# A hybrid decoder layer on one core: seven-product blocks for attention's projections, and attention moved beside pooling

## The chip, the cores and the metric

The kernel runs on one core of a Trainium2 chip. The metric is device time in microseconds (us), the median of several runs. A NeuronCore has five engines, each with its own queue in order: TensorE (PE in the profile; PEld is its weight load), VectorE (DVE), ScalarE (ACT), GpSimd (POOL) and SyncE (SP), which here issues the loads. Tiles lie in on-chip memory (SBUF, and PSUM for TensorE's sums); DRAM is reached by DMA.

## The reference, cut to what matters

One layer, 512 positions, model width 2048, float32:

```
h    = rms_norm(x) * norm_g
proj = h @ w_in            # columns: z_ssd 2048 | x 2048, B 512, C 512 | dt 32 | u_pool 2048 | z_pool 2048
                           #          | q 1536 | k 1536 | v 1536 | z_attn 512 | gate logits 3 x 2048
y_ssd  = ssd_branch(z_ssd, conv(x,B,C), dt, ...)                # convolution, SiLU, chunked scan, gated norm
y_pool = (pooled(u) - u) @ pool_w * pool_scale * silu(z_pool)   # causal means, windows 2, 4, 8, 16, one per group
y_attn = combine(attn(q,k,v) of 3 groups) * silu(z_attn)        # 4 heads of 128 per group, windows of 128 keys, dilation 1, 4, 16
merged = sigmoid(g0) * (y_ssd @ w_br_ssd) + sigmoid(g1) * (y_pool @ w_br_pool) + sigmoid(g2) * (y_attn @ w_br_attn)
x = x + merged @ w_out
out = x + sigmoid((rms_norm(x) * ple_norm_g) @ w_ple_gate) * (p @ w_ple_proj)
```

## The kernel before

**Precision.** Every large product is made of three matmuls in the fast float32 form. A value is split into `hi` (rounded by a copy on ScalarE, L136) and `lo`, the remainder (a subtraction on VectorE, L137); hi x hi, hi x lo and lo x hi are added in PSUM (`product`, L146). The weights are loaded as `raw` tiles of 128 x 1024 values (512 KB), three buffers deep, split, and used at once. `h` is kept transposed and split in `HT` (`hh`, `hl`) for most of the run.

**Entries, jobs and ticks.** `plan` lists all weight tiles in the order of use, an entry each; `jobs` lists the products. `split(n)` (L116) emits the split of all entries up to n and, for each, the load of the entry three further on. A job asks for the split of the entry two ahead, emits the 24 matmuls of its own entry (12 in a seven-product block), evacuates PSUM after its last entry, and calls `tick()`. `tick` (L84) takes one step of the generator at the head of `tasks` and one of the generator at the head of `other`; in this way vector work and small matmuls are laid between the large ones, in an order written out by hand. `flush()` (L89) ticks until both queues are empty, with no large matmuls between. `job_a` (L151) makes 128 positions x 512 columns with `h` as the stationary operand, `job_b` (L179) the transposed form. 512 columns over a depth of 2048 are 16 x 4 x 3 = 192 matmuls of 512 columns in either.

**Seven-product blocks** (`s_block`, L251). 1,024 columns of `w_in` are treated as a 2 x 2 block product with seven products in place of eight (Strassen's scheme in Winograd's form), 7 x 48 = 336 matmuls instead of 384. `make_left` (L226) makes the four left-hand sums S1 to S4 of `h` once, in two halves, most of it on VectorE, and one sum per half on GpSimd (L239). The right-hand sums (T2 and T3, T1, T4) are made from the raw weights on VectorE (L274, L276, L280, L283) when an entry is split, just before its rounding copy. There are three passes over the depth: (a, T2, T3), (d, T1), (c, T4); after each, `after` (L309) adds the products in `st` tiles, and calls `evac`. For the gates that is a sigmoid on ScalarE (L551) and a store from ScalarE's queue (L553) into `gate_d`.

**Order of the stages.** (1) `start`, norm and transposition of x, beside the product p @ w_ple_proj. (2) `enter` (L556) takes SBUF for the blocks (`swap`), steps `make_left`; six seven-product blocks for the gate logits; then the SBUF goes back to the pool of 52 general tiles (`T`). (3) `load_columns` (L413): per-channel vectors, nine small loads from GpSimd, two of them (L422) of `d_skip`, element by element. (4) For each of three groups q, k, v by `job_a`; norm and transposition of q and k (`qk_norm`) and the core (`attn_core`, L626: for each block of 128 queries a score step, a transposition step and a value step) run as tasks beside the following products. (5) dt, B and C with the causal convolution in `conv_evac` (L796), `dt_task`, `ssd_prep`, and the combination of the groups (`combine`, L744). (6) x of the SSD, scan (`ssd_core`), z of the SSD, z of attention (`za_evac`) beside the norm `y_norm` (L1050). (7) The SSD's merge, four `job_a`, then group 0 of pooling, attention's merge (`merge_att`, after a flush) and the rest of pooling (`pool_group`, L1137; sums in `pooled`). (8) Split of pooling's result (`yp_split`), pooling's merge, output projection, last gate, output.

The change and the prediction touch the helpers `tick`, `flush`, `split`, `make_left` and `s_block`, the stages 2 to 5, and the order in 6 to 8.

Of the kernel before, what the change touches and what calls it, by code (L numbers as in the profile page):

```python
# [9 lines left out]
F32 = mybir.dt.float32  # L10
# [7 lines left out]
L = 512  # L18
# [13 lines left out]
def hybrid_kernel(ctx: ExitStack, tc: tile.TileContext, x, p, norm_g, w_in, conv_w, conv_b, dt_bias, a_log,  # L32
# [40 lines left out]
    tasks, other = deque(), deque()  # L73
# [42 lines left out]
    def split(n):  # L116
        while state["split"] <= n and state["split"] < len(plan):
# [4 lines left out]
            if callable(plan[i]):  # L122
                r, k, c = plan[i]("raw"), 2, L
            else:
                r = raws.pop(i)
                _, k, c = plan[i]
# [6 lines left out]
            else:  # L133
                hi = wp.tile([128, k, c], F32R, name="hi", tag="hi")
                lo = wp.tile([128, k, c], F32R, name="lo", tag="lo")
                A.copy(hi, r)  # L136
                (G if 1 < i < EARLY else V).tensor_tensor(lo, r, hi.bitcast(F32), op=ALU.subtract)  # L137
# [88 lines left out]
    def make_left():  # L226
# [8 lines left out]
        for q0 in (0, 4):  # L235
            x = {}
            for n in ("L11", "L21", "L22", "L12"):
                x[n] = sp.tile([128, 4, 256], F32, name="x4", tag="t2", bufs=4)
                (G if n == "L12" else V).tensor_tensor(x[n], part(0, n), part(1, n), op=ALU.add)  # L239
            x["S3"] = sp.tile([128, 4, 256], F32, name="x4", tag="rs", bufs=2)  # L240
            V.tensor_sub(x["S3"], x["L11"], x["L21"])
            V.tensor_add(x["L22"], x["L21"], x["L22"])
            V.tensor_sub(x["L11"], x["L22"], x["L11"])
            V.tensor_sub(x["L12"], x["L12"], x["L11"])
            for n, o in (("S2", "L11"), ("S3", "S3"), ("S4", "L12"), ("S1", "L22")):
# [3 lines left out]
            yield  # L249

    def s_block(c0, evac):  # L251
# [15 lines left out]
        def entry(name, e, loads):  # L267
            def f(what):
# [3 lines left out]
                elif what == "raw":  # L272
                    if name == "T2":
# [3 lines left out]
                        raw["T2", e], raw["T3", e] = t, raw.pop(("b", e))  # L277
                        raw.pop(("a", e)), raw.pop(("d", e))
                    elif name == "T1":
                        V.tensor_sub(raw["d", e], raw["d", e], raw["T2", e])  # L280
                        return raw["d", e]
                    elif name == "T4":
                        V.tensor_sub(raw["T2", e], raw["T2", e], raw["c", e])  # L283
                        return raw["T2", e]
                    return raw[name, e]
                elif name in ("T3", "T1", "T4", "c"):
                    raw.pop(({"T1": "d", "T4": "T2"}.get(name, name), e))
                    if name == "T4":
                        raw.pop(("c", e), None)
            if name == "c":  # L290
                keep = f

                def f(what):
                    if what != "done":
                        return keep(what)
# [10 lines left out]
        def tile_():  # L306
            return held["sp"].tile([128, L], F32, name="st", tag="st", bufs=8)

        def after(name):  # L309
            for t in range(2):  # L310
                p = ps[name][t]
                if name == "L11":
                    st["u2", t] = tile_()
# [3 lines left out]
                elif name == "S3":  # L317
                    st["u3", t] = tile_()
# [3 lines left out]
                elif name == "S1":  # L322
                    o = tile_()
# [4 lines left out]
                elif name == "L12":  # L328
                    evac(t, 0, p, tile_())
# [83 lines left out]
    def load_columns():  # L413
# [10 lines left out]
        yield  # L424
        yield
# [14 lines left out]
    gb = []  # L440
# [7 lines left out]
    def start():  # L448
# [30 lines left out]
        load_xt(3)  # L479

# [63 lines left out]
    hook(flush)  # L544


    gate_d = dram.tile([3, L, D], F32, name="gate_d")

# [6 lines left out]

    def enter():  # L556
        swap("sp")
        load(state["split"])
        split(state["split"])
        tasks.append(make_left())  # L560
        step(tasks)

    hook(enter)
    for br in (0, 2, 1):
# [3 lines left out]
    hook(lambda: tasks.append(load_columns()))  # L568
# [23 lines left out]
    def qk_evac(raw, ss):  # L592
        def f(t, ps):
            q, sq = T("q"), T("sq")
            A.copy(q, ps)
            G.tensor_tensor(sq, q, q, op=ALU.mult)
            V.tensor_reduce(ss[:, 4 * t:4 * t + 4], sq.rearrange("q (h d) -> q h d", h=4), axis=AX.X, op=ALU.add)
            raw[t] = q
        return f
# [26 lines left out]
    def attn_core(gi, t0):  # L626
        yield from fresh(t0, 2)
# [65 lines left out]
        if gi == 2:  # L693
            other.append(combine())

    sm_mx = sm(4)
# [6 lines left out]

    def v_perm(gi):
        def f(kt, t):
            if gi == 0:
                return hkt(kt, t)
            return tuple(HT[i][:, kt].rearrange("q (i r) -> q r i", r=4)[:, t] for i in range(2))
        return f

    def v_evac(gi):
        def f(t, ps):
            v = T("v")
            if t % 2:
                V.tensor_copy(v, ps)
            else:
                A.copy(v, ps)
            vv[gi, t] = v
        return f

    def attention(gi):
        rq, rk = {}, {}
        job_a(w_in, QO + gi * L, 16, hkt, qk_evac(rq, ss16),
              post=lambda: tasks.append(qk_norm(gi, rq, ss16, rt16, scr16, qT, False)))
        job_a(w_in, KO + gi * L, 16, hkt, qk_evac(rk, ss16b),
              post=lambda: tasks.append(qk_norm(gi, rk, ss16b, rt16b, scr16b, kT, True)))
        job_a(w_in, VO + gi * L, 16, v_perm(gi), v_evac(gi), post=lambda: tasks.append(attn_core(gi, now["t"])))

    for gi in range(3):
        attention(gi)  # L730

    za_d = dram.tile([4, 128, L], F32, name="za_d")
    ya_d = dram.tile([4, 128, L], F32, name="ya_d")

    def za_evac(j):
        def f(n, ps):
            z = T("za")
            A.activation(z, ps, AF.Silu)
            nc.scalar.dma_start(out=za_d[2 * j + n], in_=z)
        return f  # L740
# [576 lines left out]
```

## Time and profile before

| | |
|---|---|
| median of 3 runs | 2753.78 us (2751.42 to 2754.65) |
| the profiled execution | 2756.26 us; its span, first to last instruction, 2753.4 us |
| mean granted TensorE clock | 0.986 |
| 1,024 columns of gates (336 matmuls), one block | 83.8 to 84.0 us |
| VectorE, ScalarE, GpSimd busy | 49%, 34%, 8% of the span |
| DMA | 326.5 MB, mean 119 GB/s |

How to read the rows: a row of the timeline gives start, duration, engine, source line, operation, output <- input, shapes, and in brackets the engine's idle time before it and what ended that. A row of the view by windows gives a stretch, then the busy time and the number of instructions of each engine, the granted clock (PEclk, 1.00 is full), the DMA engines' busy share and GB/s. A row of the view of waits gives who waited for whom, the sum in us, how many times, and the longest. In a row of the view by lines, what stands before the bar is line, engine, operation, tiles, shapes and count; behind it come busy time, mean ns of one, and the idle time before. A row of DMA issues gives their count, the KB of each, and the median us to landing.

### The profile page before, as it was taken

Reading aid. Unit: us, or ns where it says so; the run is one execution under the profiler, and the core shown is the slowest. Engines: PE = TensorE matmul, PEld = TensorE weight load, DVE = VectorE, ACT = ScalarE, POOL = GpSimd, SP = SyncE. Lnnn points to the kernel's source line nnn. Section 1 sums busy time; section 2 is a strip of 40 time slices with the busy share of each in tenths; the row PEclk is TensorE's granted clock in tenths of the full one; section 3 lists DMA queues with packets and bytes.
Section 4 is the critical chain, followed back from the end, with each engine's and each line's share of the span. In section 5 each row is a group of like instructions: output and inputs, shape, how many; then the busy total and the mean of one; then the engine's idle time right before and its main releaser. Section 6 shows DMA issues by size and latency. Waiting matters only on the chain.

```text
span 2753.4 us, 30122 instructions
## 1 busy us (share of the span) xinstructions
PE 2668.3 (97%) x12086; PEld 2203.5 (80%) x12086; DVE 1351.7 (49%) x1718; ACT 926.1 (34%) x1223; POOL 223.8 (8%) x204
## 2 busy tenths in 40 slices
PE   6799999999999999999999999999999999999999
PEld 5577777778889897878888888878888888788887
DVE  7777677653243335577765442352443543333333
ACT  4344344433233334434443321222222322223322
POOL 4000000001000000031111210030000001100000
PEclk9899999999999999999999999999999999999999
DMA  5355445563323332374443343453333333333343
GB/s 199 100 168 160 137 139 146 159 124 100 92 85 85 88 85 71 85 189 125 119 127 85 92 146 111 141 153 100 94 98 99 95 123 115 112 107 123 110 158 99
DMA packets 218067, 326.52 MB, mean 119 GB/s; under 512 B 14796, under 2 KB 103688, under 8 KB 217928
## 3 DMA queue, kind: packets, MB, share of 16 engines
q1 hardware_dynamic: 208552, 306.01, 37.6%
q10 hardware_dynamic: 7488, 13.63, 1.3%
q0 software_dynamic: 1888, 4.97, 1.1%
q8 instruction: 94, 1.54, 0.2%
q14 instruction: 45, 0.37, 0.0%
HBM read 301.34 MB, written 23.22 MB: 118 GB/s over the span
## 4 chain that ended last, share of the span: by engine, by line
PE 86%; DVE 7%; ACT 4%; issue 2%; ACTq 0%; DMA 0%; POOL 0%; SPq 0%; DVEq 0%
PE pg L147 24%; PE pg L148 24%; PE pg L149 24%; PE pg L348 10%; ACT hi L136 2%; DVE lo L137 2%; ACT st L551 1%; PE ps L990 1%; PE ps L681 0%; DVE t L276 0%; DVE cv L802 0%; DVE rs L274 0%; PE ps L649 0%; DVE x L239 0%; ACTq L553 0%
## 5 line engine op out<-in xcount | busy, mean ns | idle before, releaser
L137 DVE TENSOR_TENSOR lo<-raw,hi 128x1024 fp32r<-128x1024 f32 x465 | 571.8, 1233 | 960.5 <-ACT hi L136 956.9
L136 ACT CAST hi<-raw 128x1024 fp32r<-128x1024 f32 x468 | 488.5, 1050 | 951.6 <-PE pg L149 558.3
L147 PE MATMUL pg<-hh,hi 128*128 128x512 f32 x1216 | 485.0, 399 | 0.0
L148 PE MATMUL pg<-hl,hi 128*128 128x512 f32 x1216 | 474.5, 390 | 0.0
L149 PE MATMUL pg<-hh,lo 128*128 128x512 f32 x1216 | 474.3, 390 | 0.0
L147 PEld LDWEIGHTS pg<-hh,hi 128*128 128x128 f32 x1216 | 229.0, 188 | 51.6 <-issue 4.8
L148 PEld LDWEIGHTS pg<-hl,hi 128*128 128x128 f32 x1216 | 229.0, 188 | 48.8 <-issue 3.1
L149 PEld LDWEIGHTS pg<-hh,lo 128*128 128x128 f32 x1216 | 228.8, 188 | 48.3
L147 PE MATMUL pg<-hi,hh 128*128 128x512 f32 x576 | 229.6, 399 | 0.0
L149 PE MATMUL pg<-hi,hl 128*128 128x512 f32 x576 | 225.6, 392 | 0.0
L148 PE MATMUL pg<-lo,hh 128*128 128x512 f32 x576 | 225.5, 391 | 0.0
L348 PE MATMUL pg<-hi,hh 128*128 128x512 f32 x288 | 118.3, 411 | 22.1 <-ACT hi L136 22.1
L149 PEld LDWEIGHTS pg<-hi,hl 128*128 128x128 f32 x576 | 124.0, 215 | 17.5
L148 PEld LDWEIGHTS pg<-lo,hh 128*128 128x128 f32 x576 | 124.3, 216 | 16.6
L147 PEld LDWEIGHTS pg<-hi,hh 128*128 128x128 f32 x576 | 124.1, 215 | 16.6
L348 PE MATMUL pg<-lo,hh 128*128 128x512 f32 x288 | 118.4, 411 | 9.4 <-DVE lo L137 6.7
L348 PE MATMUL pg<-hi,hl 128*128 128x512 f32 x288 | 116.7, 405 | 0.0
L1094 POOL TENSOR_TENSOR g<-g 128x512 f32<-128x512 f32 x32 | 47.2, 1506 | 743.2 <-DVE g L1090 743.2
L136 ACT CAST hi<-t 128x1024 fp32r<-128x1024 f32 x48 | 50.4, 1050 | 151.4 <-DVE t L276 82.8
L149 PE MATMUL pg<-hi,ypl 128*128 128x512 f32 x256 | 99.8, 390 | 1.0 <-DVE ypl L385 1.0
L147 PE MATMUL pg<-hi,mh 128*128 128x512 f32 x256 | 100.5, 393 | 0.0
L147 PE MATMUL pg<-hi,yph 128*128 128x512 f32 x256 | 100.1, 391 | 0.0
(351 smaller groups left out, 4321.5 us busy)
## 6 DMA issues: line engine op xcount, KB each, us to landing
raw<-in_w_in_dram SPq DMA_DIRECT2D x320, 512.0 KB, 3.8
raw<-in_w_br_ssd_dram SPq DMA_DIRECT2D x32, 512.0 KB, 3.8
raw<-in_w_br_pool_dram SPq DMA_DIRECT2D x32, 512.0 KB, 3.7
raw<-in_w_out_dram SPq DMA_DIRECT2D x32, 512.0 KB, 3.8
raw<-in_w_ple_gate_dram SPq DMA_DIRECT2D x32, 512.0 KB, 3.8
rs<-in_w_in_dram SPq DMA_DIRECT2D x24, 512.0 KB, 3.7
gate_d<-st ACTq DMA_DIRECT2D x48, 256.0 KB, 2.4
g<-gate_d SPq DMA_DIRECT2D x48, 256.0 KB, 5.0
```

Of the source, the lines that this page charges most:

```text
L136: A.copy(hi, r)
L137: (G if 1 < i < EARLY else V).tensor_tensor(lo, r, hi.bitcast(F32), op=ALU.subtract)
L147: PE.matmul(ps, lhsT=lh, rhs=rh, start=first, stop=False)
L148: PE.matmul(ps, lhsT=lh, rhs=rl, start=False, stop=False)
L149: PE.matmul(ps, lhsT=ll, rhs=rh, start=False, stop=last)
L348: PE.matmul(ps[name][t], lhsT=lh, rhs=r[:, k], start=first and i == 0, stop=last and i == 2, skip_group_check=name in ("L11", "L12"))
L551: A.activation(o, src, AF.Sigmoid)
L990: PE.matmul(pd[q, rows(h // 2)], lhsT=xdt[:, h * 64:h * 64 + 64], rhs=bc[h // 4][:, rows(h % 4)], start=True, stop=True)
L1094: G.tensor_tensor(m[t, j], m[t, j], g, op=ALU.add)
```

## The change

- `split` calls a new step `mix` of an entry (the right-hand sums) one entry earlier: after the rounding copy of an entry the sums of the next one are emitted, and only then the entry's own remainder. T1 gets a tile of its own.
- `make_left` runs wholly on VectorE and yields six times per half instead of once.
- dt and the eight tiles of B and C come first, right after the norm, with `make_left` as a task beside them; they are stored to DRAM (`dt_d`, `bc_d`).
- q, k, v and z of attention, 5,120 columns, are five more seven-product blocks, ahead of the six for the gates. Their results go to `qkv_d` in DRAM, by stores from ScalarE's queue.
- `load_columns` is issued in `start`; its transposition is done before the blocks.
- A third queue of tasks is stepped by every tick. Pooling follows the gates; attention (`attn_all` in `other`) and the preparation (`prep_all` in `third`: norms of q and k, dt, B and C) run beside it, and load what they need from DRAM. What is left of both is done in a `flush_all` after pooling. `flush` waits for `tasks` alone.
- The groups' results go to `oo_d`; `combine` runs beside z of the SSD, loads them, transposes z of attention and makes attention's split result.
- Merges in the order attention, SSD, pooling. `y_norm` runs beside attention's merge, all its remainders on VectorE. Pooling's result goes to `yp_d` and is loaded and split beside the end of the SSD's merge (`yp_stream`); one quarter of the merged sum is kept in `m_d` between the merges.

The diff, cut to its core:

```diff
@@ tick, flush
         step(tasks)
         step(other)
+        step(third)
 
     def flush():
-        while tasks or other:
+        while tasks:
+            tick()
+
+    def flush_all():
+        while tasks or other or third:
             tick()
@@ split
             if callable(plan[i]):
+                plan[i]("mix")
                 r, k, c = plan[i]("raw"), 2, L
...
                 A.copy(hi, r)
+                if state["dma"] > i + 1 and callable(plan[i + 1]):
+                    plan[i + 1]("mix")
                 (G if 1 < i < EARLY else V).tensor_tensor(lo, r, hi.bitcast(F32), op=ALU.subtract)
@@ make_left
-                (G if n == "L12" else V).tensor_tensor(x[n], part(0, n), part(1, n), op=ALU.add)
+                V.tensor_tensor(x[n], part(0, n), part(1, n), op=ALU.add)
+                if n in ("L21", "L12"):
+                    yield
@@ start
         load_xt(3)
+        vab.append(load_columns())
@@ stage order
+    def qkv_evac(c0):
+        def f(t, half, src, o):
+            if src is not o:
+                A.copy(o, src)
+            c = c0 - QO + half * L
+            nc.scalar.dma_start(out=qkv_d[rows(t), c:c + L], in_=o)
+        return f
...
+    for ct in range(16, 24, 2):
+        job_b(w_in, XBC + ct * 128, 16, hk, conv_evac(ct, st_tile))
+    hook(flush)
+    for b in range(5):
+        s_block(QO + 1024 * b, qkv_evac(QO + 1024 * b))
-    for br in (0, 2, 1):
+    for br in (2, 0, 1):
         for j in (0, 2):
             s_block(GATES + br * D + j * L, gate_evac(br, j))
@@ attention as tasks
+    def fetch_qkv(name, gi):
+        r = {}
+        for t in range(4):
+            r[t] = T(name)
+            nc.sync.dma_start(out=r[t], in_=qkv_src(name, gi, t))
+        return r
+
+    def qk_prep(name, gi, dst):
+        ss, rt, tmp = (ss16, rt16, scr16) if name == "q" else (ss16b, rt16b, scr16b)
+        raw = fetch_qkv(name, gi)
+        yield
+        yield
+        for t in range(4):
+            sq = T("sq")
+            G.tensor_tensor(sq, raw[t], raw[t], op=ALU.mult)
+            V.tensor_reduce(ss[:, 4 * t:4 * t + 4], sq.rearrange("q (h d) -> q h d", h=4), axis=AX.X, op=ALU.add)
+            if t % 2:
+                yield
+        yield from qk_norm(gi, raw, ss, rt, tmp, dst, name == "k")
+
+    def prep_all():
+        for gi in range(3):
+            while at["begun"] < gi - 1:
+                yield
+            yield from qk_prep("q", gi, qT)
+            while at["done"] < gi - 1:
+                yield
+            yield from qk_prep("k", gi, kT)
+            at[gi] = True
+        yield from dt_task()
+        yield from ssd_prep()
+
+    def attn_all():
+        for gi in range(3):
+            while gi not in at:
+                yield
+            at["begun"] = gi
+            yield from attn_core(gi)
+            at["done"] = gi
@@ combine
+            ps, z = PS(), T("za")
+            for t in range(4):
+                PE.transpose(ps[:, rows(t)], za[t][:, rows(h)], ident)
+            A.activation(z, ps, AF.Silu)
...
+            V.tensor_mul(o, o, z)
+            a, b = T("yah", F32R), T("yal", F32R)
+            split_to(a, b, o)
@@ pooling and after
+    hook(lambda: (third.append(prep_all()), other.append(attn_all())))
     for g in range(4):
         pool_group(g)
+    hook(flush_all)
...
+    hook(lambda: other.append(combine()))
     for kt in range(0, 16, 2):
         job_b(w_in, Z_SSD + kt * 128, 16, hk, z_evac(kt))
...
+    hook(lambda: other.append(y_norm()))
+    merge(2, w_br_attn, 4, lambda kt: Yah[kt], True)
+    hook(lambda: (at.update(merge0=True), step(other)))
+    merge(0, w_br_ssd, 16, lambda kt: (Yh[kt], Yl[kt]), False, last=lambda: other.append(yp_stream()))
...
-    merge(1, w_br_pool, 16, lambda kt: Yph[kt], False, pre=flush, after=lambda j: tasks.append(m_turn(j)))
+    merge(1, w_br_pool, 16, lambda kt: Yph[kt], False, after=lambda j: tasks.append(m_turn(j)))
```

More of the change, by code (lines that the diff above doesn't have):

```diff
@@ L624, in qk_norm, with attn_core @@
                 yield
[L626 to L627 removed]
+    def attn_core(gi):
+        for t, v in fetch_qkv("v", gi).items():
+            vv[gi, t] = v
+        yield
+        yield
         nm, den = stat[gi]
@@ L692, in attn_core @@
             yield
-        if gi == 2:
-            other.append(combine())
+        for h in range(4):
+            G.dma_start(out=oo_d[gi, h], in_=oo[gi, h])
+    oo_d = dram.tile([3, 4, 128, L], F32, name="oo_d")
     sm_mx = sm(4)
@@ L702, in hybrid_kernel @@
     hook(make_masks)
[L704 to L740, printed above, removed]
     w_d = dram.tile([12, L], F32, name="w_d")
@@ L888, in hybrid_kernel, with ssd_prep @@
     btok, cbm = {}, {}
-    def ssd_prep(t0):
-        yield from fresh(t0, 2)
+    def ssd_prep():
+        for j in range(4):
+            for i in (16 + j, 20 + j):
+                conv[i] = T("cv")
+                nc.sync.dma_start(out=conv[i], in_=bc_d[i - 16])
+        yield
+        yield
         for j in range(4):
@@ new lines, in hybrid_kernel, with y_norm @@
+    for kt in range(0, 16, 2):
+        job_b(w_in, Z_SSD + kt * 128, 16, hk, z_evac(kt))
+    def y_norm():
+        yield
+        s, r, v = sq_sum["t"], T("r"), T("v")
+        ps = PS()
+        PE.matmul(ps, lhsT=dts["one"], rhs=s, start=True, stop=True)
+        V.tensor_scalar(v, ps, 1.0 / D, EPS, op0=ALU.mult, op1=ALU.add)
+        A.activation(s, v, AF.Sqrt)
+        for i in range(4):
+            V.reciprocal(r[:, rows(i)], s[:, rows(i)])
+        V.tensor_mul(s, r, r)
+        V.tensor_mul(s, s, v)
+        V.tensor_scalar(s, s, -0.5, 1.5, op0=ALU.mult, op1=ALU.add)
+        V.tensor_mul(r, r, s)
+        yield
@@ new lines, in hybrid_kernel, with load_gates, merge, ev @@
+    m, gs, MT = {}, {}, {}
+    m_d = dram.tile([L, L], F32, name="m_d")
+    def load_gates(br, j, ts=range(4)):
+        for t in ts:
+            if j == 3 and (t, 3) not in m and br != 2:
+                m[t, 3] = T("m")
+                nc.sync.dma_start(out=m[t, 3], in_=m_d[rows(t), :])
+            gs[t, j] = T("g")
+            nc.sync.dma_start(out=gs[t, j], in_=gate_d[br, rows(t), j * L:(j + 1) * L])
+    def merge(br, w, kn, xk, first, last=None, after=None):
+        def ev(j):
+            def f(t, ps):
+                g = gs.pop((t, j))
+                V.tensor_mul(g, g, ps)
+                if first and j == 3:
+                    G.dma_start(out=m_d[rows(t), :], in_=g)
+                elif first:
+                    m[t, j] = g
+                else:
+                    G.tensor_tensor(m[t, j], m[t, j], g, op=ALU.add)
+            return f
+        for j in range(4):
+            job_a(w, j * L, kn, lambda kt, t: tuple(a[:, rows(t)] for a in xk(kt)), ev(j),
+                  pre=lambda j=j: (last() if last and j == 3 else None, load_gates(br, j, range(3 if (br, j) == (1, 0) else 4))),
+                  post=(lambda j=j: after(j)) if after else None)
```

293 lines of the change are left out of this document (121 added, 172 removed).

## The prediction

> **What bounds the kernel now.** I read the page first, then TensorE's timeline, the stage windows, the waits, and last the timelines around the longest waits.
>
> ```profile
> span 2753.4 us, 30122 instructions
> PE 2668.3 (97%) x12086; PEld 2203.5 (80%) x12086; DVE 1351.7 (49%) x1718; ACT 926.1 (34%) x1223; POOL 223.8 (8%) x204
> ```
>
> ```profile
> 322.79 0.63 PE L348 MATMUL pg<-hi,hh 128*128 128x512 f32 x1
> 323.22 0.63 PE L348 MATMUL pg<-lo,hh 128*128 128x512 f32 x1
> ...
> 609.58 0.40 PE L149 MATMUL pg<-hi,hl 128*128 128x512 f32 x1
> ...
> 622.28 0.39 PE L148 MATMUL pg<-lo,hh 128*128 128x512 f32 x1
> ```
>
> TensorE is busy for 97% of the span, but that hides its pace. The last two timeline rows are the first and the last of 57 consecutive 512-column matmuls: 12.70 us over 56 steps, 0.2268 us each (0.39 us is the length of one; they overlap). The first two rows, from just after a wait, stand 0.43 apart: a slow clock. So a stage has a floor, its count times 0.2268, and above it lie small matmuls, waits and slow clock. By the loops the program holds 10,976 matmuls of that width: 2,489 of the 2,753 us. Fewer of them is time saved one for one; all else must come out of the other 264.
>
> ```profile
> core 0: us, PE busy (x) PEld busy (x) DVE busy (x) ACT busy (x) POOL busy (x), PEclk, DMA share, GB/s
> 57.40:97.50 40.10, 14.44 (x37) 9.91 (x37) 35.59 (x27) 10.81 (x11) 12.20 (x4) 0.63 0.29 91
> 97.50:591.20 493.70, 469.23 (x1979) 377.54 (x1980) 349.93 (x330) 205.62 (x225) 0.00 (x0) 0.97 0.49 147
> 591.20:1023.50 432.30, 431.77 (x2024) 376.59 (x2023) 154.83 (x220) 141.41 (x228) 34.53 (x39) 1.00 0.36 91
> 1023.50:1137.20 113.70, 110.03 (x533) 89.17 (x532) 54.55 (x85) 52.92 (x96) 5.70 (x5) 0.98 0.28 76
> 1870.40:2197.00 326.60, 326.60 (x1442) 270.46 (x1441) 129.81 (x193) 84.32 (x100) 0.00 (x0) 1.00 0.35 97
> ```
>
> The stages: the start of the gates; the rest of the gates (seven-product blocks); q, k, v with attention inside; dt, B, C and the end of attention; most of pooling. Above the floor lie 40.1 - 37 x 0.2268 = 31.7 us; 493.7 - 1979 x 0.2268 = 44.9, or 7.6 for each block of 336; 432.3 - 1728 x 0.2268 = 40.4; 113.7 - 416 x 0.2268 = 19.4 (these two mostly small matmuls); pooling sits on its floor. It is in the seven-product blocks that TensorE really waits, and the view of waits says for whom:
>
> ```profile
> PE pg L348 <- ACT hi L136: 34.8, 9, 12.7
> PE pg L348 <- DVE lo L137: 11.4, 18, 1.9
> ...
> PE ps L427 <- DMA raw<-in_w_in_dram: 0.5, 1, 0.5
> ```
>
> The rounding copy on ScalarE (hi) and its remainder on VectorE (lo) come late; a weight load ends a wait once, for 0.5 us.
>
> **The change, term by term.**
>
> *Fewer matmuls.* q, k, v (1,728) and z of attention (192) become five blocks of 1,024 columns at 7 x 48 = 336: 1,680. 240 x 0.2268 = **-54.4 us**.
>
> *The start.* From 57.4 to 97.5 us TensorE waits while VectorE and GpSimd make the left-hand sums. Now dt, B and C (32 + 384 matmuls, 94 us) run over these, cut into twelve steps and all on VectorE.
>
> ```profile
> 10.23 1.23 DVE L137 TENSOR_TENSOR lo<-raw,hi 128x1024 fp32r<-128x1024 f32 x1 [0.97 <-ACT hi L136]
> ```
>
> ```profile
> L802 DVE SCALAR_TENSOR_TENSOR cv<-pg,cols,cv 128x511 f32<-128x511 f32 (+2 forms) x19 | 14.2, 748 | 8.8 <-ACT cv L800 8.4
> ```
>
> The sums are 2 x 13 operations of the first row's size, 26 x 1.23 = 32 us; with 24 x 0.75 = 18 of convolution and 16 x 1.23 = 20 of remainders VectorE has 70 of 94 us: covered. Were it not, the 31.7 would come back in part. TensorE still begins cold; at 0.43 a matmul I charge 2.7. So 31.7 - 2.7 = **-29.0**.
>
> But the columns' small loads move from 600 us to the start. What they do to the DMA engines:
>
> ```profile
> 604.88 1.67 POOL L422 DMA_DIRECT2D cols<-in_d_skip_dram  x2
> ```
>
> ```profile
> 609.00:627.00 18.00, 18.00 (x81) 14.90 (x80) 3.66 (x5) 2.11 (x2) 0.00 (x0) 1.00 0.81 15
> ```
>
> ```profile
> 15.25 2.36 SPq L411 DMA_DIRECT2D x<-in_x_dram  x4
> 33.15 1.05 ACT L136 CAST hi<-raw 128x1024 fp32r<-128x1024 f32 x1
> ```
>
> The two loads of d_skip, element by element, keep the engines 81% busy for 18 us in which 15 GB/s move: nearly nothing for anyone else. TensorE did not feel it there. In the new place they are issued after the first remainder (10.23 + 1.23) and seven other small issues, about 16 us into the run, and act some 3 us later, when the last quarter of x (issued from 15.25) and the last weights of the first product are under way. ScalarE uses those from 33.15. If the jam lasts from 19 to 38, that copy slips by 6 us and the chain of x with it; if it also catches the weights before, by 18; if it begins only when x is through, by nothing. I take **+6**, 0 to 18. The Trainium skill, DMA: Bandwidth & Descriptors, section Queues, rings and completion order, says that an engine goes round its queues and switches between packets. By that rule x would slip through between two slow packets at about +3; the row with 15 GB/s speaks against it.
>
> *Stalls of the seven-product blocks.* The worst is at the change to the third pass:
>
> ```profile
> 315.17 0.63 ACT L551 ACTIVATE st<-st 128x512 f32<-128x512 f32 x1 [1.89 <-DVE st L324]
> 315.84 0.33 ACTq L553 DMA_DIRECT2D gate_d<-st  x1
> ...
> 319.42 1.04 ACT L136 CAST hi<-raw 128x1024 fp32r<-128x1024 f32 x1 [0.45 <-ACT st L551]
> ```
>
> ```profile
> 320.51 0.80 PE L348 MATMUL pg<-hi,hh 128*128 128x512 f32 x1 [2.23 <-ACT hi L136]
> 321.77 0.80 PE L348 MATMUL pg<-lo,hh 128*128 128x512 f32 x1 [0.47 <-DVE lo L137]
> ```
>
> Four sigmoids and their stores, 4.25 us, stand ahead of the next hi on ScalarE's queue; TensorE waits 2.2 us for hi, about 1 for lo, then runs slow for a while. The change calls the weight mixing one entry early, ahead of the previous remainder on VectorE instead of behind it. That frees VectorE some 1.7 us sooner for the sums that the sigmoids read. In gate blocks the sigmoids stay: the wait for hi falls to 0.6, that for lo stays at 1.0. The block's other stalls (7.6 less some 5.4 here, say 2.0) stay, for there too a hi stands behind evacuations on ScalarE, and the mixing now comes ahead of a lo. With 0.6 for the clock: 1.6 + 2.0 + 0.6 = 4.2. In q, k, v, z blocks these evacuations are stores alone, 0.33 each without the 0.63, so hi is 2.5 us earlier and in time: I leave 1.0. Together 6 x 4.2 + 5 x 1.0 = 30.2 against 44.9: **-14.7** (between 11 x 0.5, -39, and 11 x 7.6, +39).
>
> Whether the clock falls after such short gaps, one more place tells:
>
> ```profile
> 1820.47 0.50 PE L147 MATMUL pg<-hi,yah 128*128 128x512 f32 x1 [0.84 <-ACT hi L136]
> 1821.73 0.50 PE L148 MATMUL pg<-lo,yah 128*128 128x512 f32 x1 [0.76 <-DVE lo L137]
> 1823.08 0.63 PE L149 MATMUL pg<-hi,yal 128*128 128x512 f32 x1
> ```
>
> Gaps of 0.84 and 0.76 were followed by matmuls of 0.63, as at 322.79, so the 0.6 stands. The Trainium skill's TensorE: Matmul & The Clock Gate, Part 1, has the clock fall only after an idle window of about 3.4 us; by it the six gate blocks would be 3.6 us cheaper in all, and these rows contradict it.
>
> *Attention beside pooling.*
>
> ```profile
> L653 DVE TENSOR_TENSOR e<-ps,mask 128x512 f32<-128x512 f32 x4 | 2.8, 690 | 10.1 <-PE ps L649 10.1
> L662 ACT ACTIVATE e<-e,st_more 128x128 f32<-128x128 f32 x16 | 6.2, 390 | 11.9 <-DVE st_more L657 11.9
> L668 PE MATMUL ps<-ident,e 128*128 128x128 f32 x16 | 2.6, 276 | 0.0
> L671 ACT COPY et<-ps 128x512 f32<-128x512 f32 x4 | 2.3, 580 | 3.3 <-PE ps L668 3.3
> ```
>
> Its small matmuls (within the 40.4 + 19.4) move at the same price. z of attention is now turned by 16 transposes, at most 2.6 / 16 = 0.16 us each: **+2**. Attention, its norms, dt and the preparation of B and C step beside pooling's vector work, up to three queues a tick; a tick is 24 matmuls or 5.44 us. VectorE's load over the stage's 1,728 matmuls, from the windows: attention 154.8 - 72 x 1.23 = 66, dt and preparation 54.6 - 17 x 1.23 - 18 = 16, pooling with its remainders 129.8 x 1728 / 1442 = 156: 238 of 392 us, no bound on average. But where the sums of windows 8 and 16 meet mask, maximum and norm, a tick holds 7 to 9 us, and the exponentials that the next tick's transposes need slip. A dozen such ticks at 0.7 us: **+8** (0 to 35).
>
> Counting the yields, attention and preparation need 78 ticks; pooling gives 72. The last two query blocks of group 2 run in the closing flush with nothing over them: mask and maximum 0.69 each, four exponentials at 0.39 and a read of their sums, a copy of 0.58, some 4.5 us a block. Two of these, part of it under the preparation's small matmuls, and a cold start after: **+9**.
>
> *The back end.*
>
> ```profile
> 1801.40:1826.90 25.50, 23.90 (x98) 19.04 (x97) 17.14 (x32) 7.45 (x10) 3.35 (x3) 0.93 0.41 124
> ```
>
> ```profile
> raw<-in_w_in_dram SPq DMA_DIRECT2D x320, 512.0 KB, 3.8
> ```
>
> The window holds the flush ahead of attention's merge: 25.5 - 96 x 0.2268 = 3.7 us above the floor, which goes, as does the split of pooling's result in one go (1 us). y_norm moves beside the first merge with all 16 remainders on VectorE, 0.69 each; I let that cost 4. The loads of o, z, m and pooling's result stand in SP's queue among weights that land in 3.8 us and were late once: 0. **-1** (-5 to +15).
>
> *Sum.* -54.4 - 29.0 + 6 - 14.7 + 2 + 8 + 9 - 1 = -74. The profiled execution took 2756.3 us, 2.9 more than its span; with the change 2682. The median of the runs, 2753.8, lies 2.5 below it, so I predict 2680.
>
> **The rivals.**
>
> - *Stalls stay in every block.* hi goes on waiting. Eleven blocks at 7.6, 53 us more than I have: 2733. Against: five blocks have no sigmoid. Chance 0.08.
> - *Attention becomes a chain beside pooling.* Each of its 36 steps waits one us for a vector engine that pooling holds, 36 in place of 8: 2708. For: the bunching. Against: attention now costs 40.4 us for 2024 - 1728 = 296 small matmuls, 0.14 each, nearly their bare price. 0.15.
> - *Nothing collides.* No jam, no bunching, the flush covered: 2680 - 6 - 8 - 9 = 2657. 0.10.
> - *Slower: the weight queue is held up.* The 45 new loads of pooling (36 tiles of q, k, v, 9 of B, C, dt) stand in SP's queue ahead of weights, and one that waits for a free tile holds every weight behind it. Weights are asked for two ticks or 10.9 us ahead, and need 3.8 to land and 2.3 for hi and lo: from a wait of 4.8 us on TensorE stalls. To lose 80 us each of the 45 must wait 6.6: 2760. Against: one raw-weight wait of 0.5 us in the whole run. 0.03.
>
> **How the numbers follow.** My forecast, 2660 to 2700 on its own, has 0.64. The range 2648 to 2722 takes in the second and the third rival and leaves out the first and the last. About 0.2%, 5.5 us, is what a measurement here can tell from no change; only the last rival and a bad case of the first come near it: faster 0.95, same 0.02, slower 0.03.
>
> **What would show it.** Right: TensorE without a hole between 60 and 100 us; q, k, v, z blocks 77 us apart, gate blocks 80; no wait for hi of over 1.5 us in the former; a hole of some 7 us where pooling ends. Wrong: dense work beginning after 70 us, raw weights among TensorE's releasers, or pooling 30 us above its floor and its small matmuls.

## The result, and the profile after

The changed kernel took 2689.3 us (median of 4 runs, 2687.5 to 2689.8) against 2754.0 before: a ratio of 0.9766, 95% interval 0.9749 to 0.9783. It is 64.7 us faster where 74 were forecast. The profiled execution took 2689.67 us, 1.7 more than its span. From its page, the span and the engines:

```profile
span 2688.0 us, 30282 instructions
PE 2608.4 (97%) x11862; PEld 2139.7 (80%) x11862; DVE 1555.3 (58%) x1925; ACT 1000.2 (37%) x1282; POOL 210.6 (8%) x219
```

TensorE is as full as before, at 97%; again only the stages tell where time is lost. The windows of the changed kernel, cut at the first wide matmul of each stage: dt, B and C; q, k, v and z of attention; the gates; pooling with attention; x and z of the SSD.

```profile
58.30:153.50 95.20, 94.77 (x420) 76.43 (x419) 68.80 (x69) 37.76 (x43) 2.41 (x1) 1.00 0.44 130
153.50:539.30 385.80, 382.26 (x1682) 314.91 (x1681) 297.40 (x282) 159.35 (x163) 0.00 (x0) 1.00 0.53 162
539.30:1011.70 472.40, 463.50 (x2018) 377.16 (x2017) 353.34 (x335) 210.77 (x227) 0.00 (x0) 1.00 0.52 157
1011.70:1501.30 489.60, 457.50 (x2159) 379.68 (x2158) 238.03 (x417) 188.90 (x316) 46.40 (x76) 0.97 0.40 119
1501.30:1920.10 418.80, 407.09 (x2019) 328.73 (x2018) 273.23 (x430) 172.96 (x215) 70.73 (x57) 0.99 0.44 128
```

The stage of x and z of the SSD was not shown of before; there it is

```profile
1137.00:1546.60 409.60, 405.88 (x2026) 329.48 (x2025) 261.66 (x426) 166.84 (x206) 67.29 (x58) 0.99 0.44 122
```

From each length the stage's wide matmuls (416, 1,680, 2,016, 1,728 and 1,536 of them) at 0.2268 us are taken off. What is left, in us:

| term | before | after | change | forecast |
|---|---|---|---|---|
| wide matmuls, 10,976 to 10,736 | 2489.4 | 2434.9 | -54.4 | -54.4 |
| start of the dense work: 31.7 of stall; after, 0.9 in dt, B, C and the start 0.9 later | 31.7 | 1.8 | -29.9 | -29.0 + 6 |
| seven-product blocks (after: 4.8 + 15.2) | 44.9 | 20.0 | -24.9 | -14.7 |
| attention and the SSD's x and z (before 40.4 + 19.4 + 61.2; after 97.7 + 70.4) | 121.0 | 168.1 | +47.1 | +2 + 8 + 9 |
| all behind that (2753.4 - 1546.6 - 5,184 wide; 2688.0 - 1920.1 - 3,264 wide) | 31.1 | 27.6 | -3.5 | -1 |

The sum is -65.6, the spans differ by 65.4. So the total is close by luck, because two errors offset one another: blocks and start came out 17 better, attention beside pooling 28 worse. TensorE's longest waits say the same:

```profile
PE ps L770 <- ACT e L764: 17.6, 4, 8.5
...
PE pg L353 <- DVE lo L145: 9.6, 15, 0.8
PE ps L711 <- ACT et L773: 5.6, 2, 5.4
PE ps L856 <- DVE eb L1038: 5.5, 1, 5.5
...
PE pg L353 <- ACT hi L142: 2.8, 7, 1.5
```

The wait for hi, 34.8 us before, has shrunk to 2.8. At the head stands a new one: attention's transposes (L770) wait for its exponentials (L764), four times, once for 8.5 us.

**The blocks.** At the change to the third pass of the first gate block, where before 2.23 us passed for hi, the timeline has now

```profile
599.56 0.49 PE L353 MATMUL pg<-hi,hh 128*128 128x512 f32 x1 [0.21 <-ACT hi L142]
600.82 0.50 PE L353 MATMUL pg<-lo,hh 128*128 128x512 f32 x1 [0.77 <-DVE lo L145]
601.16 0.40 PE L353 MATMUL pg<-hi,hl 128*128 128x512 f32 x1
601.39 0.39 PE L353 MATMUL pg<-hi,hh 128*128 128x512 f32 x1
```

0.21 for hi, 0.77 for lo, and behind them matmuls 0.23 apart: no slow stretch follows.

**The longest hole beside pooling**, in the timelines of VectorE, ScalarE and TensorE:

```profile
1295.49 2.50 DVE L704 TENSOR_TENSOR q<-q,small 128x512 f32<-128x512 f32 x4
1297.90 1.22 DVE L145 TENSOR_TENSOR lo<-raw,hi 128x1024 fp32r<-128x1024 f32 x1
...
1303.18 0.69 DVE L390 TENSOR_TENSOR pll<-q,plh 128x512 fp32r<-128x512 f32 x1 [0.68 <-ACT plh L389]
1303.79 0.68 DVE L755 TENSOR_TENSOR e<-ps,mask 128x512 f32<-128x512 f32 x1
1304.51 0.69 DVE L757 TENSOR_REDUCE small<-e 128x4 f32<-128x512 f32 x1
...
1305.48 1.28 ACT L764 ACT_TABLE_LOAD   x1 [2.33 <-DVE st_more L759]
1306.77 0.40 ACT L764 ACTIVATE e<-e,st_more 128x128 f32<-128x128 f32 x1
...
1292.29 1.05 PE L751 MATMUL ps<-kT,qT 128*128 128x128 f32 x8
...
1307.32 1.63 PE L770 MATMUL ps<-ident,e 128*128 128x128 f32 x4 [8.52 <-ACT e L764]
...
1315.18 1.12 PE L711 MATMUL ps<-ident,q 128*128 128x128 f32 x4 [5.38 <-ACT et L773]
...
1317.37 0.63 PE L155 MATMUL pg<-hh,hi 128*128 128x512 f32 x1
...
1444.25 1.63 PE L770 MATMUL ps<-ident,e 128*128 128x128 f32 x4 [5.83 <-ACT e L764]
```

TensorE made the scores at 1292.29 (L751). On VectorE the norm of the next group's q (2.50), a remainder (1.22) and a channel tile's pooled sums (from 1299.04 to 1303.79, 4.75 us) stand ahead of the mask addition at L755. Only after mask, maximum and a table load of 1.28 can ScalarE make the exponentials for which TensorE has waited 8.52 us; the copy at L773 is then late behind the next pooled sums (5.38), and the matmuls behind the hole run 0.43 apart. The last row is a second hole: there steps of dt's preparation and a late remainder stand ahead of the mask as well, behind the pooled sums.

### The profile page after: what moved, and what is told of

It reads as the page before. It is cut to its first block, busy times and chain, and to the rows that moved or that the text cites. A ratio compares the mean times of both kernels' runs of the same rounds, so it can differ in the third digit from the quotient of the medians.

```text
span 2688.0 us, 30282 instructions
## 1 busy us (share of the span) xinstructions
PE 2608.4 (97%) x11862; PEld 2139.7 (80%) x11862; DVE 1555.3 (58%) x1925; ACT 1000.2 (37%) x1282; POOL 210.6 (8%) x219
## 4 chain that ended last, share of the span: by engine, by line
PE 83%; DVE 8%; ACT 5%; issue 2%; DMA 1%; ACTq 1%; POOL 0%; SPq 0%; DVEq 0%
PE pg L353 27%; PE pg L155 18%; PE pg L157 18%; PE pg L156 18%; DVE lo L145 2%; ACT hi L142 2%; DMA x<-in_x_dram 1%; ACT st L565 1%; DVE bc L1015 1%; DVE s L1094 1%; PE ps L1052 0%; ACTq L567 0%; PE ps L783 0%; ACT e L764 0%; PE ps L711 0%
## 5 line engine op out<-in xcount | busy, mean ns | idle before, releaser
L145 DVE TENSOR_TENSOR lo<-raw,hi 128x1024 fp32r<-128x1024 f32 x421 | 522.4, 1242 | 674.3 <-ACT hi L142 664.4
L142 ACT CAST hi<-raw 128x1024 fp32r<-128x1024 f32 x424 | 443.6, 1050 | 810.0 <-PE pg L157 440.3
L156 PEld LDWEIGHTS pg<-hl,hi 128*128 128x128 f32 x1152 | 218.6, 190 | 45.5 <-issue 2.4
L145 DVE TENSOR_TENSOR lo<-t,hi 128x1024 fp32r<-128x1024 f32 x132 | 161.6, 1224 | 101.6 <-ACT hi L142 101.1
L353 PE MATMUL pg<-lo,hh 128*128 128x512 f32 x528 | 207.0, 392 | 8.4 <-DVE lo L145 8.4
L142 ACT CAST hi<-t 128x1024 fp32r<-128x1024 f32 x132 | 138.6, 1050 | 204.5 <-PE pg L353 165.3
L353 PE MATMUL pg<-hi,hh 128*128 128x512 f32 x528 | 206.4, 391 | 1.3 <-ACT hi L142 1.3
L353 PE MATMUL pg<-hi,hl 128*128 128x512 f32 x528 | 205.5, 389 | 0.0
L353 PEld LDWEIGHTS pg<-hi,hh 128*128 128x128 f32 x528 | 99.1, 188 | 24.8 <-ACT hi L142 4.1
L157 PE MATMUL pg<-hi,ml 128*128 128x512 f32 x256 | 100.2, 391 | 0.0
L156 PE MATMUL pg<-lo,mh 128*128 128x512 f32 x256 | 100.1, 391 | 0.0
L155 PE MATMUL pg<-hi,xh 128*128 128x512 f32 x256 | 99.8, 390 | 0.0
```

The lines of the kernel that those rows point to most:

```text
L155: PE.matmul(ps, lhsT=lh, rhs=rh, start=first, stop=False)
L156: PE.matmul(ps, lhsT=lh, rhs=rl, start=False, stop=False)
L157: PE.matmul(ps, lhsT=ll, rhs=rh, start=False, stop=last)
L353: PE.matmul(ps[name][t], lhsT=lh, rhs=r[:, k], start=first and i == 0, stop=last and i == 2, skip_group_check=name in ("L11", "L12"))
```

## The experiments

Each is the changed kernel with one edit; ratios are to the kernel before, on the same chip (medians of 2755 to 2756 us there; the changed kernel has 0.9766). "Excess" is a stage's length less its wide matmuls at 0.2268 (worked out from unrounded times, so that a last digit can differ by one).

**The gains, undone one at a time.** First, the right-hand sums are mixed where they were before, behind the remainder.

```
-                if state["dma"] > i + 1 and callable(plan[i + 1]):
-                    plan[i + 1]("mix")
```

> The right-hand sums of an entry are made when that entry is split, as before, and not one entry ahead; all else is as in the changed kernel (2689.3 us; above the floor its q, k, v, z blocks hold 4.8 us and its gate blocks 15.1). Theory one, the early sums took the stalls away: the gate blocks go back to about 7.6 us each, 45 in all, the five others to about 2 each, 10: some 35 us more, 2725. Theory two, their place does not matter and the stalls fell because GpSimd is off the sums and the stage starts warm: the two numbers stay at 5 and 15, and the time stays within 5 us of 2689.

2738.5 us, 0.9935 [0.9918, 0.9953]. Windows of q, k, v, z and of the gates, and TensorE's waits in the two together:

```profile
151.50:554.10 402.60, 389.83 (x1682) 313.41 (x1681) 296.01 (x281) 155.06 (x163) 0.00 (x0) 1.00 0.51 154
554.10:1057.30 503.20, 477.54 (x2017) 383.90 (x2016) 353.09 (x335) 208.16 (x228) 0.00 (x0) 0.98 0.49 149
```

```profile
PE pg L351 <- DVE lo L143: 18.8, 34, 0.8
PE pg L351 <- ACT hi L142: 17.6, 13, 2.2
```

Excess 21.6 and 46.0, where the changed kernel has 4.8 and 15.2. The gate blocks are back at 7.7 each, just the 7.6 of before, and so is the wait of 2.2 for hi. The five other blocks have 4.3 each, twice what was expected. Where the mixing stands is worth 47.6 us in eleven blocks, the whole gain of the blocks.

Second, q, k, v and z as ten dense jobs of 512 columns.

```
-    for b in range(5):
-        s_block(QO + 1024 * b, qkv_evac(QO + 1024 * b))
+    for b in range(10):
+        job_a(w_in, QO + L * b, 16, hkt, dense_evac(QO + L * b))
```

> q, k, v and z of attention by eight products again (ten ordinary blocks of 512 columns at the same place, results stored to DRAM as in the changed kernel); all else as in the changed kernel. Theory one, the 240 matmuls are saved one for one: +54.4 us, less the 4.8 that the seven-product blocks lie above their floor, so about +50, 2739. Theory two, the blocks give back part of it in stores, tiles or sums that the rest pays for: under +40, below 2729.

2739.1 us, 0.9939 [0.9924, 0.9953]:

```profile
153.00:588.20 435.20, 435.20 (x1921) 360.48 (x1920) 116.31 (x105) 98.08 (x103) 0.00 (x0) 1.00 0.42 124
```

435.2 in place of 385.8 us, 49.4 more: 240 matmuls are 54.4, less the 4.8 of excess that goes with the blocks. Fewer matmuls are paid one for one.

Third, the left-hand sums made before dt, B and C, with nothing over them.

```
     hook(enter)
+    hook(flush)
```

> The left-hand sums are finished with nothing over them before dt, B and C begin. Theory one, covering them was worth the whole wait: 26 operations at 1.23 us, so a hole of 32 us and a cold start of 2, about +34, 2723. Theory two, the wait before the change came mostly from the first weights, split behind GpSimd, and not from the sums: a hole under 20 us, below 2710.

2717.9 us, 0.9859 [0.9842, 0.9875], 28.6 more by the medians and 25.6 by the ratios:

```profile
57.20:86.90 29.70, 7.59 (x36) 4.22 (x34) 28.60 (x29) 9.51 (x12) 0.00 (x0) 0.69 0.03 12
```

VectorE is busy for 28.6 of the 29.7 us, and TensorE with dt alone. In the changed kernel these sums cost next to nothing: dt, B and C have 0.9 us of excess beside them.

**The jam of d_skip.** It came as forecast: the two loads issue at 15.77 and 17.34, and

```profile
20.00:40.00 20.00, 14.91 (x63) 12.33 (x62) 17.60 (x30) 9.15 (x24) 15.42 (x12) 0.83 0.99 73
```

the DMA engines are 99% busy for 73 GB/s; the last quarter of x, issued from 15.66, lands only from 39.3 to 41.3. What does it cost? First the two loads were put behind the gates in the program:

```
+    def load_d_skip():
...
     hook(lambda: swap("tp"))
+    hook(load_d_skip)
```

> The two element-by-element loads of d_skip are issued after the gates, as before; the other columns stay at the start. Theory one, the slack in the chain of x absorbs the jam of 19 to 39 us: the start (first to last wide matmul of the p product, 46.0 us) stays within 1 us, and so does the total. Theory two, the one on record, the jam costs 6 us: the start shrinks to 40 us and the time to 2683.

2697.2 us, 0.9788 [0.9774, 0.9803]: some 6 slower by the ratios, whose intervals just overlap. The loads were not where the program has them:

```profile
58.76 1.70 POOL L430 DMA_DIRECT2D cols<-in_d_skip_dram  x2
```

```profile
83.51 1.05 ACT L142 CAST hi<-raw 128x1024 fp32r<-128x1024 f32 x1 [14.92 <-DMA raw<-in_w_in_dram]
```

```profile
101.25 0.80 PE L155 MATMUL pg<-hh,hi 128*128 128x512 f32 x1 [4.65 <-ACT hi L142]
```

GpSimd has nothing to do from there until the masks of attention, so it issued them 950 us early. One weight load, issued at 59.99, then landed at 83.41, 23.4 us in place of 4, and the stage of B and C has 9.5 us of excess in place of 0.7. Half of it is the wait in the last row: its hi stands on ScalarE behind evacuations that the late weight had held up. The run does not say what the jam cost at the start; it shows what the jam does to weights. So it was taken away altogether: d_skip as 16 rows of two numbers, spread on VectorE, turned with the other columns.

```
-        for i in range(2):
-            G.dma_start(out=cols[64 * i:64 * i + 64, DSK:DSK + 16], ...
+        G.dma_start(out=vb[96:112, 256:258], in_=bass.AP(..., ap=[[2, 16], [1, 2]]))
...
+        for i in range(2):
+            V.tensor_copy(vb[96:112, 64 * i:64 * i + 64], vb[96:112, 256 + i:257 + i].to_broadcast([16, 64]))
```

> d_skip is loaded as 16 rows of two numbers, spread over 64 columns on VectorE and turned with the other columns by the transpose that is there already; the two loads that took it element by element are gone, from the start and from everywhere else. Theory one (the jam cost the start something, as the prediction had it with 6 us): DMA moves well over 100 GB/s from 20 to 40 us in place of 73, the stage up to dt begins its end earlier, dt's first matmul at 52 to 55 us in place of 58.3, and the time is 3 to 6 us shorter, 2683 to 2686. Theory two (the chain of x had slack enough for it): the bytes move earlier, but dt still begins at 57 to 59 us and the time is within 2 us of the changed kernel, ratio 0.976.

2689.2 us, 0.9761 [0.9748, 0.9775]: no difference.

```profile
20.00:40.00 20.00, 14.74 (x70) 12.18 (x68) 17.33 (x32) 11.47 (x28) 15.61 (x12) 0.91 0.85 252
```

```profile
56.04 0.32 PE L434 MATMUL ps<-ident,vb 112*128 112x112 f32 x1 [1.80 <-DVE vb L432]
...
57.81 0.63 PE L593 MATMUL pg<-hh,hi 128*64 128x512 f32 x1
```

252 GB/s in place of 73, x there by 25 us in place of 41, yet dt begins at 56.1 in place of 58.3, and B and C at 65.1 in place of 65.7: the edit's own wait of 1.80 for VectorE and 3 us of slow matmuls behind it (0.63, 0.43 apart) took most of it back. Without that wait dt would have begun at 54.3, as it did at 54.6 with the loads issued late. With the jam in place dt began at 56.3 to 59.2 in the eleven kernels that have it there, the changed one among them. So the jam is worth 2 to 5 us at dt's start, of which this way to remove it keeps 0.6, nothing in the time. The truth lies between the two theories. Why x landing 16 us later costs so little is seen on ScalarE, in the changed kernel and then with d_skip turned:

```profile
39.36 0.63 ACT L491 ACTIVATE sq<-x 128x512 f32<-128x512 f32 x1 [4.14 <-DMA x<-in_x_dram]
...
33.41 0.62 ACT L491 ACTIVATE sq<-x 128x512 f32<-128x512 f32 x1
```

ScalarE comes to the squares of x's last quarter at 33.4 us in any case, 8 us after x has landed there; so they slip by 6 and not by 16.

**Attention beside pooling.** Four edits, each against one suspected cause. Attention ahead of pooling's sums in each tick (and its preparation second):

```
     def tick():
+        if now.get("pool"):
+            step(other)
+            step(third)
+            step(tasks)
+            return
```

> While pooling runs, each tick now calls attention first, then its preparation, then pooling's own sums, so that pooling's sums stand behind attention's mask, maximum and norm on VectorE. Theory one (order on VectorE: pooled sums of some 4.8 us stand ahead of the mask addition, and the exponentials that the next transposes need slip): the stage of 1,728 wide matmuls beside pooling, 97.7 us above its floor in the changed kernel, comes down to about 85; the holes of 8.5 us (near 1307) and 5.8 us (near 1444) shrink to 4 or less; about 2677 us, ratio to before 0.972. Theory two (the step itself is too long a chain of VectorE, ScalarE with its table loads, and two small PSUM buffers, whoever goes first): the excess stays within 97.7 plus or minus 4 and the holes stay over 5 us; 2685 to 2693 us, ratio 0.976. If pooling's sums now become late for the evacuation, waits of TensorE for a pg buffer appear instead, and it is slower.

2673.9 us, 0.9699 [0.9685, 0.9714]; excess 81.3. The hole of 8.5 is 3.2, that of 5.4 is 2.7, that of 5.8 is 1.4.

```profile
1011.10:1484.30 473.20, 454.52 (x2160) 377.91 (x2158) 237.91 (x417) 189.48 (x316) 48.04 (x76) 0.98 0.41 123
```

Pooling's sums in two ticks, the order as it was:

```
# pooled, between the sums and the subtraction
+                yield
                 q = T("q")
```

> Pooling's sums of a channel tile are cut into two ticks instead of one; nothing else. Theory one (a bunch of pooled sums on VectorE in front of attention's step makes the exponentials late): the longest bunch is halved, the 8.5 us hole falls to some 6, the excess of the stage beside pooling from 97.7 to about 90; 2681 us, ratio 0.973. Theory two (attention's step is a chain of its own): excess 94 to 102 and the holes as long as they were; 2685 to 2693 us. Since pooling then needs more ticks than the stage has, the closing flush may get longer by up to 5 us, which would show past 1458 us.

2672.1 us, 0.9695 [0.9679, 0.9711]; excess 79.0. The holes of 8.5 and 5.8 are gone, that of 5.4 is 3.6; the closing flush is no longer than it was.

```profile
1304.69 1.12 PE L711 MATMUL ps<-ident,q 128*128 128x128 f32 x4 [3.57 <-ACT et L773]
```

```profile
1011.40:1482.30 470.90, 455.98 (x2159) 379.84 (x2158) 235.56 (x417) 189.77 (x316) 47.57 (x76) 0.98 0.41 124
```

The same work on VectorE (238.0, 237.9 and 235.6 us in the three kernels), 16 to 19 us less: the bunch of sums ahead of attention's step is the cause, not VectorE's load. (A yield also moves pooling's later steps by a tick; but the other edit, which moves none, shortens the same holes.) Both went below the 85 and 90 expected.

The closing flush of the changed kernel holds no wide matmul at all:

```profile
1479.40:1501.30 21.90, 14.47 (x85) 12.09 (x85) 7.33 (x16) 8.77 (x27) 3.52 (x7) 0.84 0.41 153
```

21.9 us, 7.4 of them waits, the rest small matmuls partly at low clock. Now k's preparation no longer waits for the group before:

```
-            while at["done"] < gi - 1:
-                yield
             yield from qk_prep("k", gi, kT)
```

> k's preparation no longer waits for the previous group's attention to be done, so that preparation and attention end inside the 72 ticks of pooling and no flush with nothing over it is left. Theory one (78 steps in 72 ticks: the rest runs uncovered): the wait of 7.4 us and the slow clock behind it at 1458 to 1505 go; the excess beside pooling falls from 97.7 by 9 to 12; about 2679 us, ratio 0.973. Theory two (the flush is hardly more than its 114 small matmuls, 17.6 us, which have to run somewhere): no more than 4 us less, 2685 or above. If k's steps now fall on ticks that pooling already fills, new holes in the first half would eat the gain: then the end is clean and the excess is still above 93.

2675.4 us, 0.9707 [0.9692, 0.9721]; excess 80.1: 17.6 less, more than the 9 to 12 expected.

```profile
1012.20:1484.10 471.90, 452.28 (x2159) 376.26 (x2158) 238.06 (x417) 183.27 (x313) 47.88 (x75) 0.99 0.41 124
```

Not all of that was at the end: the long holes of 8.5, 5.4 and 5.8 are 4.2, 2.8 and 3.1 here. The 85 small matmuls of the flush now run elsewhere; at 0.14 us each, the price of the prediction, that is 12 of the 21.9, so that by this estimate the flush itself loses 10.

Last, the merge of attention. In the changed kernel it runs beside the last SSD group:

```profile
1819.31 1.11 PE L1005 MATMUL ps<-ident,cv 128*128 128x128 f32 x4 [2.63 <-ACT za L857]
...
1820.65 0.63 PE L156 MATMUL pg<-hl,hi 128*128 128x512 f32 x1
...
1833.99 1.11 PE L856 MATMUL ps<-ident,z 128*128 128x128 f32 x4 [5.45 <-DVE eb L1038]
```

Transposes of one wait for a small PSUM buffer that the other still reads. VectorE reads it late (L1038, at 1833.25) because, among others, 2.8 us of the merge's own sums stand ahead of it. The z jobs there, and then the edit, which starts the merge after three of the eight z jobs:

```profile
1700.50:1920.10 219.60, 207.92 (x1030) 167.40 (x1029) 146.69 (x223) 92.91 (x119) 52.63 (x42) 0.98 0.45 131
```

```
-    hook(lambda: other.append(combine()))
     for kt in range(0, 16, 2):
+        if kt == 6:
+            hook(lambda: other.append(combine()))
```

> The merge of attention (its z, turned by transposes) starts after three of the eight z jobs, instead of beside the last SSD group. Theory one (merge and SSD core take the two small PSUM buffers from each other, and the transposes wait for a buffer that VectorE's last step of the core holds): the holes of 2.6 and 5.5 us at 1819 and 1834 go, the z stage's excess falls from 45.5 to about 36; 2680 us, ratio 0.973. Theory two (these holes come from VectorE being full, whichever stands first): the holes move to later in the stage, excess 43 to 48; 2686 to 2692 us. If the merge then does not end within the z jobs, the matmuls of attention behind it wait, and it gets slower by what is left over.

2676.2 us, 0.9708 [0.9694, 0.9723]. Both holes are gone, and the z jobs take 205.9 us in place of 219.6, an excess of 31.6 in place of 45.5:

```profile
1697.50:1903.40 205.90, 203.95 (x1032) 164.56 (x1030) 139.33 (x221) 90.29 (x117) 51.04 (x41) 1.00 0.47 137
```

That refutes a VectorE that is full whichever stands first. The edit takes the merge's transposes from the shared buffers and its sums from in front of the core's at once, and doesn't tell these two apart.

**Together.** Attention first, halves and the later merge:

> Attention first, pooling's sums in halves, and the merge later, the three together. Measured alone beside the changed kernel (pooling's excess 97.7, z's 45.5), attention first gave 81.2 there, halves 79.0, the merge later 31.6 in z. Theory one (the first two remove the same holes, those behind pooled sums): excess beside pooling 77 to 81, z 32 to 34, 2655 to 2660 us, ratio 0.964. Theory two (their gains add up, as of different causes): excess beside pooling 62 to 66, 2643 us, ratio 0.959.

2652.0 us, 0.9631 [0.9618, 0.9644]; excess beside pooling 73.0, z 31.6. Between the theories: the two edits mostly remove the same holes, and 6 to 8 us add up.

```profile
1009.60:1474.50 464.90, 452.16 (x2159) 376.90 (x2158) 234.56 (x417) 189.44 (x316) 46.98 (x76) 0.99 0.41 125
```

Halves, no wait before k, later merge:

> Pooling's sums in halves, no wait before k's preparation, and the merge later. Theory one (halves remove the holes in the middle, 18.7 us alone, the missing wait the closing flush, 17.6 us alone: places that do not overlap except for the hole near 1444): excess beside pooling 64 to 70, z 32 to 34, 2643 to 2650 us, ratio 0.960. Theory two (halves need one more tick a tile, so that the end of the stage fills up again): excess 76 to 82, 2656 to 2662 us, ratio 0.964.

2639.4 us, 0.9585 [0.9572, 0.9599].

```profile
1010.10:1463.70 453.60, 445.83 (x2160) 372.69 (x2159) 235.52 (x417) 183.84 (x313) 46.22 (x75) 1.00 0.43 129
```

Excess 61.7, which is 17.3 less than with the halves alone; in that the hole of 3.6, which is gone too, and the slow matmuls behind it are counted. No gap of over 1.3 us is left there. All four:

> Attention first, halves, no wait before k's preparation, and the merge later. Theory one (only two causes, the bunch ahead of attention's step and the uncovered end): like the combination without attention first, excess beside pooling 62 to 70, 2641 to 2650 us, ratio 0.959. Theory two (with attention first and k early, pooling's sums come last and hold TensorE's big buffers up): waits for pg buffers appear and it is 5 us or more slower than that combination.

2640.9 us, 0.9589 [0.9576, 0.9602]; excess 63.7, no wait for a pg buffer.

```profile
1012.00:1467.60 455.60, 447.69 (x2160) 373.82 (x2159) 236.29 (x417) 183.97 (x313) 46.29 (x75) 1.00 0.42 128
```

Where both edits have already removed the long holes, the missing flush is worth 9.3 (73.0 - 63.7). With halves and no flush, attention first adds nothing. The better of these, halves with no flush and the later merge, beats the kernel before by 4.15% and the changed one, by the ratio 0.9585 / 0.9766, by 1.9%.

## Why the prediction was right, and where it was not

*Fewer matmuls* (-54.4): right, shown by the dense form, 49.4 slower plus the 4.8 that the blocks cost.

*The start* (-29.0): right, shown by the sums made alone, 26 to 29 slower. The cold start of 2.7 did not come: x's transposes run right up to dt's first matmul, and dt, B and C have 0.9 us of excess in all.

*The jam* (+6): it came and it held the chain of x up, but by another step than the one named. The copy that was to slip by 6 ran at 33.90, against 33.15 before, for its weights, issued at 15.03, had landed at 30.44. What slipped by 6 is the sum of squares of x's last quarter, which waited for x; 2 to 5 of that are left at the start of dt. On how the queues share the engines the prediction was half wrong. Against the rule of the Trainium skill (DMA: Bandwidth & Descriptors, Queues, rings and completion order: an engine goes round its queues, packet by packet) it held that the jam leaves nearly nothing for others. The trace agrees with the rule: d_skip came in 32 packets of 256 bytes, in two sets of 16, which took 4.1 to 8.7 us each where a packet of 2 KB took 0.08. From 24.5 to 30.5 us, between the first set (begun at 20.4 to 20.9) and the second (at 25.8 to 30.8), some 470 KB of the other queue got through, and none of it from 21 us to 24.5 and from 30.5 to 34. That fits one turn for it between two slow packets, a turn that comes up to 8.7 us late: the last weights landed right behind the first d_skip load (30.03), x behind the second (39.15), and not at the +3 that the prediction drew from the rule.

*Stalls of the blocks* (30.2 left; 20.0 measured): the mechanism was right, late mixing brings back 7.7 a gate block. The step that was mis-sized is the 4.2 for what is left in a gate block: 15.2 / 6 = 2.5. Of that, 8.8 / 6 = 1.5 are waits (7.5 for lo and 1.3 for hi in the six); the rest lies in the steps right at these waits. The 0.6 for the clock fell: ten waits of 0.5 to 0.8 for lo stand in the six blocks, and none is followed by slow matmuls. In this the Trainium skill's TensorE: Matmul & The Clock Gate, Part 1, by which the six blocks were to be 3.6 us cheaper, was the better guide than the rows chosen against it. But an idle window of about 3.4 us is not what it took here either: waits of 2.63 and 1.80, above, were followed by slow matmuls.

*Attention beside pooling* (+2 + 8 + 9; +47.1 measured): this is the step that failed, in size: the bunching and the merge were priced far too low. With three edits the excess comes down to 61.7 beside pooling and 24.8 + 31.6 in x and z, 118.1 in all against 121.0 before: moving attention there costs nothing in itself, as the prediction said of its small matmuls. VectorE's load had been forecast to the digit (238 us; 238.0 measured), and it said nothing of this. All of the loss was collisions, in three places:
- the bunching, forecast as "a dozen such ticks at 0.7 us": 16 to 19 us by either edit, 25 by both. It was not a dozen small slips but three long waits (8.5, 5.4, 5.8), since a late exponential makes the next copy late too and lowers the clock behind.
- the closing flush, forecast at +9: 9 to 11 beside the other edits (73.0 - 63.7 with both edits of the bunch, 36 - 25 in all), 10 by the estimate above. This part was right, two query blocks and all. The 17 us that the edit gives alone, or beside the halves, are in part the long holes again.
- the merge beside the SSD, counted as 16 transposes for +2: 14 us more than that. That it meets the SSD's core, at two small PSUM buffers and on VectorE, was not in the sum at all.

*Back end* (-1; -3.5): as forecast within its bounds.

The rivals: stalls stay in every block, refuted. Attention as a chain (36 us where the forecast had 8): pooling's own loss, bunching and flush, is 97.7 - 61.7 = 36, where the forecast had 17: by size the truth lay between, but it was three long waits and an end, not one us in each of 36 steps. The weight queue held up: no raw weight is among TensorE's releasers, though the fourth experiment shows what that is like. One of the prediction's own signs of being wrong came: pooling 30 us above its floor and its small matmuls. At the 0.14 us that it gave them, the 2159 - 1728 = 431 small matmuls are 60 of the 97.7, and 37 are left.

## What to carry to other kernels

When vector work is laid beside a full TensorE, do not judge it by an engine's average load (VectorE had 238 of 490 us): look for the longest run of one task's instructions in front of another task's next link, and cut it into smaller steps; a single added yield was worth 17 us here. Check that the steps fit the ticks, for what is left over runs uncovered and at a low clock, and that two tasks which run together do not stand in each other's way at a pair of buffers or on VectorE. A load has the place that its engine's queue gives it, not the one that the program text suggests.

## What the runs showed of the hardware

- Two element-by-element loads of 4 KB each held a 512 KB weight load for 23.4 us, in place of about 4. Their packets of 256 bytes (64 values) took up to 9.0 us each there, and other queues' packets came through between them.
- Whether a short wait lowers the granted clock is not a matter of its length alone. In the changed kernel a wait of 2.59 us (at 1724.54) was followed by matmuls 0.23 apart, one of 2.63 (at 1819.31) by matmuls 0.43 apart at a granted clock of 0.50. With d_skip turned, slow matmuls began 1.1 us after dt's first, behind a wait of 1.80, and lasted some 3 us. And the same two waits of 0.98 and 1.12 us, near 1153, were followed by slow matmuls in the kernels with the halves alone and with all four edits, and by none with attention first alone.
- Each ACT_TABLE_LOAD, by which ScalarE goes over to another set of functions, took 1.28 us; for attention's exponentials there were 4 of them before and 7 beside pooling, one of them right in the chain of the longest hole.
